# A feed-forward product as seven block products of sums instead of eight blocks, with two weight sums added up by the DMA

## The chip, the cores and the metric

The kernel runs on one core of a Trainium2 chip. A core has five engines that work side by side, each from its own in-order queue: TensorE (PE, matrix products; its weight loads are listed as PEld), VectorE (DVE), ScalarE (ACT), GpSimd (POOL) and SyncE (SP, which here only issues DMAs). Matrix products add into PSUM, eight banks of 128 x 512 float32; everything else lies in SBUF, 128 partitions wide. Engines wait for each other by semaphores. A DMA can be issued from SP, ACT or POOL.

The metric is device time in microseconds of one launch, lower is better.

## The reference

One layer of a diffusion backbone in float32: a token-mixing sub-layer with three mixers, then a gated feed-forward sub-layer, on 512 tokens of width 1024. The change lies in the feed-forward part:

```python
D_MODEL = 1024
D_FF = 2816      # ((8 * 1024 // 3 + 255) // 256) * 256

def swiglu(h, w_ffn_in, w_ffn_out):
    a, b = split_cols(h @ w_ffn_in, (D_FF, D_FF))
    return (jax.nn.silu(a) * b) @ w_ffn_out

h2 = rmsnorm(x, norm2_g) * (1 + sc2) + sh2          # (512, 1024)
x = x + g2 * swiglu(h2, w_ffn_in, w_ffn_out)        # w_ffn_in (1024, 5632), w_ffn_out (2816, 1024)
return rmsnorm(x, final_g)
```

## The kernel before

**Number format.** Matrix products run on float32r operands. To keep float32 accuracy each operand is split into a high and a low part (`split`, L142: ACT casts to the high part on L143, DVE subtracts it on L144), and a product is three matmuls: high x high, high x low, low x high (`mm3`, L254 to L257). The hidden state is split once; each weight tile is split after its load (`prep_w`, L146) into a pair `wh`, `wl`, of which there are two. So a third tile can be split only when the first has been used up.

**Weights.** A weight tile is 128 x 4 x 256: four blocks of 128 rows of the contraction, 256 output columns, 512 KB. `load_w` (L136, DMA on L139 by SP) brings it into one of three `wf` buffers.

**The stages around the change.** The output projection of the mixers (`gemm_tm` with `w_o`) yields token blocks m = 0 to 3, one after the other. For each, `residual` (L997) adds it to the stream `xr` and gets the norm's factor, DVE scales to `xn`, TensorE transposes `xn` (eight 128 x 128 transposes, L1032), and DVE and ACT evacuate the transposes with scale and shift (L1036, L1038). The result, features in the partitions and tokens along the free axis, is split into `h2h` and `h2l`.

**First feed-forward product.** Eleven groups g, each 256 columns of the gate half a and the matching 256 of the half b. A group takes four weight tiles (a or b, first or second half of the 1024 features), and each tile meets all 512 tokens: for two column blocks q and four row blocks kk three matmuls of 512 columns, 96 a group. Only group 0 is cut into two token halves with matmuls of 256 columns, since its second half of tokens comes last. ACT takes the SiLU of a from PSUM (L1077), DVE multiplies by b (L1078), and the product is split at once into `Ga` or `Gb`.

**Second feed-forward product.** `gemm_tm` with `w_ffn_out`: 22 row blocks k, each with a load, a scale by g2 (L154), a split and 24 matmuls. The final norm and the stores follow.

**Order.** Instructions are ordered when the program is built, by priorities: what stands under `prio("prep")` (loads, splits of weights) goes ahead as early as its buffers allow. On each engine the order is then fixed, and an instruction that waits holds up all behind it.

Of the kernel before, what the change touches and what calls it, by code (L numbers as in the profile page):

```python
# [9 lines left out]
F32 = mybir.dt.float32  # L10
# [64 lines left out]
def body(tc, I, out):  # L75
# [3 lines left out]
    with es:  # L79
# [22 lines left out]
        def gbank(name="g"):  # L102
            return psg.tile([128, 512], F32, name=name, tag="g")
# [703 lines left out]
        def cvf():  # L807
            return pF.tile([128, 512], F32, name="cvf", tag="cv", bufs=3)
# [212 lines left out]
        h2h = pH.tile([128, 8, 512], F32R, name="h2h", tag="hh")  # L1021
        h2l = pH.tile([128, 8, 512], F32R, name="h2l", tag="hl")
        for m, ps in gemm_tm(I["w_o"][0], g1b, lambda k, ms: (mh[:, k, ms], ml[:, k, ms]), 8, extra, 1):
            rs_ = residual(ps, xr, m, [xn[:, m % 2, 512 * n:512 * n + 512] for n in range(2)])
            V.tensor_scalar(out=xn[:, m % 2], in0=xr[:, m], scalar1=rs_, scalar2=None, op0=ALU.mult)
            for k4 in range(2):
                px = dbank()
                hf = cvf()
                p3, h3 = (t.rearrange("p (k j) -> p k j", k=4) for t in (px, hf))
                for kk in range(4):  # L1030
                    k = 4 * k4 + kk
                    T.transpose(p3[:, kk], xn[:, m % 2, 128 * k:128 * k + 128], ident)  # L1032
                for kk in range(4):
                    k = 4 * k4 + kk
                    if kk % 2:
                        A.activation(out=h3[:, kk], in_=p3[:, kk], func=AF.Identity, scale=a2[:, k:k + 1], bias=sh2[:, k:k + 1])  # L1036
                    else:
                        V.tensor_scalar(out=h3[:, kk], in0=p3[:, kk], scalar1=a2[:, k:k + 1], scalar2=sh2[:, k:k + 1], op0=ALU.mult, op1=ALU.add)  # L1038
                ms = slice(128 * m, 128 * m + 128)
                split(h3, h2h[:, 4 * k4:4 * k4 + 4, ms], h2l[:, 4 * k4:4 * k4 + 4, ms])  # L1040
        fstack.close()


        pG = es.enter_context(tc.tile_pool(name="pG", bufs=1))
        Ga = pG.tile([128, 18, 2, 512], F32R, name="Ga")
        Gb = pM.tile([128, 4, 2, 512], F32R, name="Gb", tag="M16")
        Gt = [Ga[:, k] for k in range(18)] + [Gb[:, k] for k in range(4)]
        gw = pM.tile([128, 2, 2, 4, 256], F32R, name="gw", tag="C16")
        wfi = I["w_ffn_in"][0].rearrange("(k p) f -> p k f", p=128)
        H2 = (lambda k: h2h[:, k], lambda k: h2l[:, k], 512, gbank)  # L1050
        cvg = lambda: pG.tile([128, 512], F32, name="cvg", tag="cv", bufs=3)
        for g in range(11):
            if g == 0:

                ab = [[gbank() for _ in range(2)], [gbank(), tbank()]]
                wts = []
                for i in range(2):
                    for half in range(2):
                        dst = None
                        if i:  # L1060
                            dst = [gw[:, half, p] for p in range(2)]
                        wts.append(prep_w(load_w(wfi[:, 4 * half:4 * half + 4, 2816 * i:2816 * i + 256]), dst=dst))
# [12 lines left out]
            for q in range(2):
                sa = cvg()
                A.activation(out=sa, in_=pa_[q], func=AF.Silu)  # L1077
                V.tensor_tensor(out=sa, in0=pb_[q], in1=sa, op=ALU.mult)  # L1078
                split(sa, Gt[2 * g + q][:, 0], Gt[2 * g + q][:, 1])
        fgb = pM.tile([128, 1024], F32, name="fgb", tag="C16")  # L1080
        GP.dma_start(out=fgb, in_=I["final_g"].partition_broadcast(128))
        yos = pH.tile([128, 4, 1024], F32, name="yos", tag="hh")
        ex = pH.tile([128, 2, 2, 4, 256], F32R, name="ex", tag="hl")
        extra = [(ex[:, i, 0], ex[:, i, 1]) for i in range(2)]
        for m, ps in gemm_tm(I["w_ffn_out"][0], g2b, lambda k, ms: (Gt[k][:, 0, ms], Gt[k][:, 1, ms]), 22, extra):
            yo = yos[:, m]
            rs_ = residual(ps, xr, m, [cvg() for _ in range(2)])
# [19 lines left out]
```

## Time and profile before

| | us |
|---|---|
| median of 3 runs | 975.82 (973.52 to 976.12) |
| profiled execution, its own time | 972.6 |
| its span, first to last instruction | 970.8 |
| first feed-forward product | 241.73 (601.20 to 842.93) |
| of it DVE busy, ACT busy | 88.67, 74.92 |
| second product and end, up to 963.80 | 120.87 |

The span is what the profile's rows cover; the execution's own time is a little longer. In a view of stretches a row gives the stretch, its length, and per engine the busy time with the number of instructions, then TensorE's granted clock, the DMA share and GB/s. In a timeline a row gives start, length, engine, line, operation, output and inputs, shape; a bracket tells how long the engine was idle before and who released it. In the view of groups the last numbers are total busy time, mean ns of one, and the idle time before. Matmuls overlap, so the time one costs in a stream is read from the distance between starts.

### The profile page before, as it was taken

What the parts mean: (1) busy time and instruction counts of PE and PEld (TensorE: products, weight loads), DVE (VectorE), ACT (ScalarE), POOL (GpSimd) and SP (SyncE); (2) the same over time, 40 slices, a digit from 0 to 9 for tenths busy, and PEclk for the clock granted to TensorE, in tenths of its full rate; (3) what the DMA queues carried; (4) which work ended last, traced back from release to release, by engine and by line L of the source; (5) the groups of instructions that cost most, each with busy time, mean ns of one, the idle gap of its engine ahead of it and who ended that gap; (6) DMA issues with size and microseconds to landing.
All of it is one profiled execution on the core that took longest, in us unless ns stands there. A gap on an engine that the chain in (4) does not pass through costs nothing.

```text
span 970.8 us, 14622 instructions
## 1 busy us (share of the span) xinstructions
PE 953.0 (98%) x5964; PEld 784.9 (81%) x5964; DVE 544.4 (56%) x880; ACT 417.9 (43%) x729; POOL 28.8 (3%) x47
## 2 busy tenths in 40 slices
PE   8999999899999999999999999999999999999997
PEld 7587887778788888888878888988888888888885
DVE  3575888369765423788874977333333333434455
ACT  5363884687863334362234346332323232211224
POOL 1002200000000000000000000000000000000000
PEclk9999999999999999999999999999999999999999
DMA  9820542512202232837774352223233333232322
GB/s 336 285 66 4 133 131 83 136 45 55 57 23 65 87 109 69 306 110 270 252 237 158 103 173 62 69 87 105 92 100 95 95 102 89 91 103 89 106 87 87
DMA packets 96836, 115.30 MB, mean 119 GB/s; under 512 B 18124, under 2 KB 84032, under 8 KB 96768
## 3 DMA queue, kind: packets, MB, share of 16 engines
q1 hardware_dynamic: 88192, 109.01, 35.5%
q0 software_dynamic: 1632, 3.44, 1.7%
q10 hardware_dynamic: 6944, 1.91, 0.8%
q8 instruction: 47, 0.77, 0.3%
q14 instruction: 21, 0.17, 0.1%
HBM read 110.58 MB, written 3.77 MB: 118 GB/s over the span
## 4 chain that ended last, share of the span: by engine, by line
PE 45%; DMA 3%; DVE 2%; issue 0%; ACT 0%; DVEq 0%
PE g L257 12%; PE g L256 12%; PE g L255 11%; PE d L257 2%; PE d L256 2%; PE d L255 2%; DMA wf<-in_w_ffn_out_dram 2%; DVE wl L144 1%; PE t L257 1%; PE t L256 1%; PE t L255 1%; DMA wm<-in_w_mod_dram 1%; DMA wf<-in_w_gate_dram 1%; DVE wf L154 1%; PE d L1032 0%
## 5 line engine op out<-in xcount | busy, mean ns | idle before, releaser
L144 DVE TENSOR_TENSOR wl<-wf,wh 128x1024 fp32r<-128x1024 f32 x131 | 160.0, 1222 | 214.4 <-ACT wh L143 213.7
L143 ACT CAST wh<-wf 128x1024 fp32r<-128x1024 f32 x131 | 137.8, 1053 | 299.1 <-PE g L256 161.5
L257 PE MATMUL g<-hh,wl 128*128 128x512 f32 x368 | 146.2, 397 | 0.3 <-DVE wl L144 0.3
L256 PE MATMUL g<-hl,wh 128*128 128x512 f32 x368 | 146.0, 397 | 0.0
L255 PE MATMUL g<-hh,wh 128*128 128x512 f32 x368 | 145.8, 396 | 0.0
L255 PE MATMUL g<-h2h,wh 128*128 128x512 f32 (+1 forms) x352 | 133.6, 380 | 0.0
L257 PE MATMUL g<-h2h,wl 128*128 128x512 f32 (+1 forms) x352 | 133.5, 380 | 0.0
L256 PE MATMUL g<-h2l,wh 128*128 128x512 f32 (+1 forms) x352 | 133.5, 379 | 0.0
L257 PEld LDWEIGHTS g<-hh,wl 128*128 128x128 f32 x368 | 69.6, 189 | 14.3 <-DVE wl L144 0.7
L256 PEld LDWEIGHTS g<-hl,wh 128*128 128x128 f32 x368 | 69.6, 189 | 14.1 <-issue 0.5
L255 PEld LDWEIGHTS g<-hh,wh 128*128 128x128 f32 x368 | 69.5, 189 | 13.6 <-issue 0.2
L256 PEld LDWEIGHTS g<-h2l,wh 128*128 128x128 f32 x352 | 66.2, 188 | 12.6
L255 PEld LDWEIGHTS g<-h2h,wh 128*128 128x128 f32 x352 | 66.2, 188 | 12.5
L257 PEld LDWEIGHTS g<-h2h,wl 128*128 128x128 f32 x352 | 66.1, 188 | 12.4
L154 DVE TENSOR_TENSOR wf<-wf,g2b 128x1024 f32<-128x1024 f32 x22 | 27.0, 1225 | 55.1 <-DMA wf<-in_w_ffn_out_dram 55.0
L830 DVE SCALAR_TENSOR_TENSOR acc<-wm,ct,acc 128x1024 f32<-128x1024 f32 x32 | 41.0, 1282 | 15.5 <-DMA acc<-in_b_mod_dram 7.3
L256 PE MATMUL d<-wl,Ga 128*128 128x512 f32 x72 | 28.0, 390 | 0.0
L257 PE MATMUL d<-wh,Ga 128*128 128x512 f32 x72 | 28.0, 389 | 0.0
L255 PE MATMUL d<-wh,Ga 128*128 128x512 f32 x72 | 28.0, 389 | 0.0
L713 ACT ACTIVATE SJ<-SJ,eGl 128x128 f32<-128x128 f32 x80 | 25.2, 403 | 3.9 <-PE d L701 3.5
L143 ACT CAST Ga<-cvg 128x512 fp32r<-128x512 f32 x18 | 11.1, 619 | 25.4 <-DVE cvg L1078 25.4
L256 PE MATMUL g<-wl,Ga 128*128 128x512 f32 x54 | 21.2, 393 | 0.1
(464 smaller groups left out, 1704.9 us busy)
## 6 DMA issues: line engine op xcount, KB each, us to landing
wm<-in_w_mod_dram SPq DMA_DIRECT2D x48, 512.0 KB, 5.5
wf<-in_w_ffn_in_dram SPq DMA_DIRECT2D x44, 512.0 KB, 3.5
wf<-in_w_in_dram SPq DMA_DIRECT2D x31, 512.0 KB, 3.9
wf<-in_w_gate_dram SPq DMA_DIRECT2D x24, 512.0 KB, 3.7
wf<-in_w_ffn_out_dram SPq DMA_DIRECT2D x22, 512.0 KB, 3.5
wf<-in_w_o_dram SPq DMA_DIRECT2D x8, 512.0 KB, 3.6
xl<-in_x_dram SPq DMA_DIRECT2D x4, 512.0 KB, 5.3
wf<-in_w_sc_out_dram SPq DMA_DIRECT2D x4, 512.0 KB, 3.3
```

What stands on the lines that cost most here:

```text
L143: A.copy(out=hi, in_=f)
L144: V.tensor_tensor(out=lo, in0=f, in1=hi.bitcast(F32), op=ALU.subtract)
L154: V.tensor_tensor(out=w, in0=w, in1=scale, op=ALU.mult)
L255: T.matmul(ps, lhsT=lh, rhs=rh, start=start, stop=False)
L256: T.matmul(ps, lhsT=lh, rhs=rl, start=False, stop=False)
L257: T.matmul(ps, lhsT=ll, rhs=rh, start=False, stop=stop)
L713: A.activation(out=S[:, u ^ par, h], in_=S[:, u ^ par, h], func=AF.Copy, scale=eGl[:, u, c_:c_ + 1])
L830: V.scalar_tensor_tensor(out=acc, in0=w, scalar=ct[:, k, 0:1], in1=acc, op0=ALU.mult, op1=ALU.add)
```

## The change

The product `w_ffn_in` x h2 of each group is treated as 2 x 2 blocks times 2 x 2 blocks. The weight blocks are A11, A12 (columns of a; first and second half of the features) and A21, A22 (columns of b). The activation blocks are B11, B21 (first 256 tokens; first and second half of the features) and B12, B22 (last 256 tokens). Instead of eight block products there are seven, of sums of blocks, each `prod` with 24 matmuls of 256 columns. In each group, in this order on TensorE:

| product | weight | activations | into |
|---|---|---|---|
| 1 | v = A11 | B11 | bank X |
| 2 | t = A21 + A22 | T1 = B12 - B11 | bank bA |
| 3 | t + v | T2 = B22 - T1 | bank bD |
| 4 | v + A21 | T3 = B12 - B22 | bank bB |
| 5 | A12 | B21 | bank X |
| 6 | t + v + A12 | -B22 | bank bA |
| 7 | A22 | T4 = B21 - T2 | bank bB |

The signs are as the code has them: c12 is stored negated and turned in its SiLU, and the products of c22 and c21 follow from it.

Weight sums: A21 + A22 and v + A21 are made by a DMA from POOL that adds into SBUF (`acc_w`, L1102); t + v and t + A12 by DVE (`add_w`, L1106), 128 x 1024 each. v and t exist twice, for even and odd groups. Loads per group rise from four tiles to six. The results are put together by seven DVE operations of 512 columns and four ACT operations, and the gated product is kept unsplit (`Gq`); it is split during the second product, into four slots `gs`. The sums of activations are made as the token blocks m = 2, 3 arrive (`sums_b`). For groups 0 and 1 products 1 and 5 run ahead of all others, since they need only the first 256 tokens.

```diff
+        def sums_b(h1, h2, js):
+            t1 = tmp()
+            V.tensor_tensor(out=t1, in0=h1, in1=Bf[:, 0:4, js], op=ALU.subtract)
+            split_b(t1, "T1", js)
+            t2 = tmp()
+            V.tensor_tensor(out=t2, in0=h2, in1=t1, op=ALU.subtract)
+            split_b(t2, "T2", js)
+            t3 = tmp()
+            V.tensor_tensor(out=t3, in0=h1, in1=h2, op=ALU.subtract)
+            split_b(t3, "T3", js)
+            V.tensor_tensor(out=Bf[:, 4:8, js], in0=Bf[:, 4:8, js], in1=t2, op=ALU.subtract)
+            nb = OB["nB22"]
+            A.activation(out=nb[:, 0, :, js], in_=h2, func=AF.Copy, scale=-1.0)
+            V.scalar_tensor_tensor(out=nb[:, 1, :, js], in0=h2, scalar=-1.0, in1=nb[:, 0, :, js].bitcast(F32), op0=ALU.mult, op1=ALU.subtract)
...
+        def prod(bank, w, b, first, last):
+            for q in range(2):
+                o, cs = bank[:, 256 * q:256 * q + 256], slice(128 * q, 128 * q + 128)
+                for kk in range(4):
+                    mm = ((w[0], b[:, 0]), (w[0], b[:, 1]), (w[1], b[:, 0]))
+                    for i, (l_, r_) in enumerate(mm):
+                        T.matmul(o, lhsT=l_[:, kk, cs], rhs=r_[:, kk], start=first and q == kk == i == 0, stop=last and kk == 3 and i == 2, skip_group_check=True)
+        def acc_w(w, src):
+            with prio("prep"):
+                GP.dma_start(out=w, in_=src, accum_op=ALU.add)
+        def add_w(w, other):
+            with prio("prep"):
+                V.tensor_tensor(out=w, in0=w, in1=other, op=ALU.add)
...
         for g in range(11):
-            if g == 0:
...
-                (pa_,) = gemm_fm(wfi[:, :, 256 * g:256 * g + 256], (H2,))
-                (pb_,) = gemm_fm(wfi[:, :, 2816 + 256 * g:2816 + 256 * g + 256], (H2,))
-            for q in range(2):
-                sa = cvg()
-                A.activation(out=sa, in_=pa_[q], func=AF.Silu)
-                V.tensor_tensor(out=sa, in0=pb_[q], in1=sa, op=ALU.mult)
-                split(sa, Gt[2 * g + q][:, 0], Gt[2 * g + q][:, 1])
+            v, t = vts[g % 2]
+            load_w2(wsrc(1, 0, g), t)
+            acc_w(t, wsrc(1, 1, g))
+            load_w2(wsrc(0, 0, g), v)
+            if g < 2:
+                X, e1 = Xs[g], e01[g]
+            else:
+                X, e1 = gbank(), e1g
+                prod(X, prep_w(v), OB["B11"], True, False)
+                A.copy(out=e1, in_=X)
+            bA = gbank()
+            prod(bA, prep_w(t), OB["T1"], True, False)
+            A.copy(out=e5, in_=bA)
+            add_w(t, v)
+            bD = dbank()
+            prod(bD, prep_w(t), OB["T2"], True, True)
+            V.tensor_tensor(out=u2, in0=bD, in1=e1, op=ALU.subtract)
+            acc_w(v, wsrc(1, 0, g))
+            bB = gbank()
+            prod(bB, prep_w(v), OB["T3"], True, False)
+            V.tensor_tensor(out=e57, in0=bB, in1=e5, op=ALU.add)
+            V.tensor_tensor(out=c22, in0=u2, in1=e57, op=ALU.add)
+            a12 = load_w(wsrc(0, 1, g))
+            if g >= 2:
+                prod(X, prep_w(a12), OB["B21"], False, True)
+            A.activation(out=sa0, in_=X, func=AF.Silu)
+            add_w(t, a12)
+            prod(bA, prep_w(t), OB["nB22"], False, True)
+            V.tensor_tensor(out=c12, in0=u2, in1=bA, op=ALU.add)
+            A.activation(out=sa1, in_=c12, func=AF.Silu, scale=-1.0)
+            prod(bB, prep_w(load_w(wsrc(1, 1, g))), OB["T4"], False, True)
+            V.tensor_tensor(out=c21, in0=u2, in1=bB, op=ALU.add)
+            V.tensor_tensor(out=Gq[g][:, :, 256:512], in0=q2(c22), in1=q2(sa1), op=ALU.mult)
+            V.tensor_tensor(out=Gq[g][:, :, 0:256], in0=q2(c21), in1=q2(sa0), op=ALU.mult)
...
-        for m, ps in gemm_tm(I["w_ffn_out"][0], g2b, lambda k, ms: (Gt[k][:, 0, ms], Gt[k][:, 1, ms]), 22, extra):
+        for m, ps in gemm_tm(I["w_ffn_out"][0], g2b, g_of, 22, extra):
```

The order on DVE inside the first product, before, over one group in the middle (`wl` is a weight split, `cvg` the product of the gate, `Ga` its split):

```order
L144 TENSOR_TENSOR wl_6071<-wf_6068,wh_6070 128x1024
L1078 TENSOR_TENSOR cvg_6056<-g_5994,cvg_6056 128x512
L144 TENSOR_TENSOR Ga_5703<-cvg_6056,Ga_5703 128x512
L1078 TENSOR_TENSOR cvg_6061<-g_5995,cvg_6061 128x512
L144 TENSOR_TENSOR wl_6101<-wf_6098,wh_6100 128x1024
L144 TENSOR_TENSOR Ga_5703<-cvg_6061,Ga_5703 128x512
L144 TENSOR_TENSOR wl_6133<-wf_6130,wh_6132 128x1024
L144 TENSOR_TENSOR wl_6163<-wf_6160,wh_6162 128x1024
```

And now, from the split for product 1 of group 3 to the split for its product 6 (`vt_5736` is v, `vt_5737` is t, `wf_6538` is A12; `Gq_5727` and the sum from `g_6286` belong to group 2; the rows of `tmps` that read `d_6476` and `g_6507` make u2 and e57):

```order
L144 TENSOR_TENSOR wl_6417<-vt_5736,wh_6416 128x1024
L1163 TENSOR_TENSOR Gq_5727<-tmps_5724 128x2x256
L1161 TENSOR_TENSOR tmps_5724<-tmps_5724,g_6286 128x512
L1164 TENSOR_TENSOR Gq_5727<-tmps_5724 128x2x256
L144 TENSOR_TENSOR wl_6447<-vt_5737,wh_6446 128x1024
L1106 TENSOR_TENSOR vt_5737<-vt_5737,vt_5736 128x1024
L144 TENSOR_TENSOR wl_6478<-vt_5737,wh_6477 128x1024
L1106 TENSOR_TENSOR vt_5737<-vt_5737,wf_6538 128x1024
L144 TENSOR_TENSOR wl_6509<-vt_5736,wh_6508 128x1024
L1146 TENSOR_TENSOR tmps_5724<-d_6476,tmps_5724 128x512
L144 TENSOR_TENSOR wl_6541<-wf_6538,wh_6540 128x1024
L1150 TENSOR_TENSOR tmps_5724<-g_6507,tmps_5724 128x512
```

What moved: four splits a group have become seven, the sum t + v (first L1106 row) stands behind the last sum and product of the group before and the split for product 2, and the split for product 4 (`wl_6509`) reads v after the DMA has added into it. The DMA is issued behind that first L1106 row.

The order on DVE at the start of the first product, before, from the last residual (`xr`) to the end of the splits of the last token block:

```order
L1003 TENSOR_TENSOR xr_5300<-xr_5300,d_5320 128x512
L144 TENSOR_TENSOR wl_5719<-wf_5716,wh_5718 128x1024
L144 TENSOR_TENSOR h2l_5312<-cvf_5618,h2h_5311 128x4x128
L1005 TENSOR_TENSOR n_r_5666<-n_s_5665 128x1
L144 TENSOR_TENSOR h2l_5312<-cvf_5630,h2h_5311 128x4x128
L1007 RECIPROCAL n_r_5666<-n_r_5666 128x1
L1025 TENSOR_SCALAR xn_5310<-xr_5300,n_r_5666 128x1024
```

And now, from the same residual to the same `xn` (`tb` are the sums T1 to T3 before their split, `ob` and `obt` the split parts):

```order
L1003 TENSOR_TENSOR xr_5300<-xr_5300,d_5322 128x512
L1038 TENSOR_TENSOR tb_5635<-cvf_5616,c16_5314 128x512
L1050 SCALAR_TENSOR_TENSOR ob_5312<-cvf_5626,ob_5312 128x4x128
L1041 TENSOR_TENSOR tb_5639<-cvf_5626,tb_5635 128x512
L144 TENSOR_TENSOR obt_5313<-tb_5635,obt_5313 128x4x128
L1047 TENSOR_TENSOR c16_5314<-c16_5314,tb_5639 128x4x128
L144 TENSOR_TENSOR obt_5313<-tb_5639,obt_5313 128x4x128
L1044 TENSOR_TENSOR tb_5643<-cvf_5616,cvf_5626 128x512
L1005 TENSOR_TENSOR n_r_5675<-n_s_5674 128x1
L144 TENSOR_TENSOR ob_5312<-tb_5643,ob_5312 128x4x128
L1007 RECIPROCAL n_r_5675<-n_r_5675 128x1
L1055 TENSOR_SCALAR xn_5310<-xr_5300,n_r_5675 128x1024
```

What moved: two splits and a weight split ahead of `xn` have become eight 512-wide operations. On TensorE the transposes of this `xn` stand behind product 1 of group 0, and ahead of product 1 of group 1.

More of the change, by code (lines that the diff above doesn't have):

```diff
@@ L1025, in body @@
             V.tensor_scalar(out=xn[:, m % 2], in0=xr[:, m], scalar1=rs_, scalar2=None, op0=ALU.mult)
+            js = slice(128 * (m % 2), 128 * (m % 2) + 128)
+            hs = []
             for k4 in range(2):
                 px = dbank()
-                hf = cvf()
-                p3, h3 = (t.rearrange("p (k j) -> p k j", k=4) for t in (px, hf))
+                p3 = px.rearrange("p (k j) -> p k j", k=4)
+                h3 = Bf[:, 4 * k4:4 * k4 + 4, js] if m < 2 else cvf().rearrange("p (k j) -> p k j", k=4)
+                hs.append(h3)
                 for kk in range(4):
@@ L1038, in body @@
                         V.tensor_scalar(out=h3[:, kk], in0=p3[:, kk], scalar1=a2[:, k:k + 1], scalar2=sh2[:, k:k + 1], op0=ALU.mult, op1=ALU.add)
-                ms = slice(128 * m, 128 * m + 128)
-                split(h3, h2h[:, 4 * k4:4 * k4 + 4, ms], h2l[:, 4 * k4:4 * k4 + 4, ms])
+                if m < 2:
+                    split_b(h3, ("B11", "B21")[k4], js)
+            if m >= 2:
+                sums_b(*hs, js)
         fstack.close()
         pG = es.enter_context(tc.tile_pool(name="pG", bufs=1))
-        Ga = pG.tile([128, 18, 2, 512], F32R, name="Ga")
@@ new lines, in prod @@
+        def prod(bank, w, b, first, last):
[4 more added lines that the diff above has]
+                    for i, (l_, r_) in enumerate(mm):
+                        T.matmul(o, lhsT=l_[:, kk, cs], rhs=r_[:, kk], start=first and q == kk == i == 0,
+                                 stop=last and kk == 3 and i == 2, skip_group_check=True)
@@ new lines, in acc_w, with load_w2, ahead @@
+        def acc_w(w, src):
[4 more added lines that the diff above has]
+                V.tensor_tensor(out=w, in0=w, in1=other, op=ALU.add)
+        def load_w2(src, w):
+            with prio("prep"):
+                SY.dma_start(out=w, in_=src)
+            return w
+        def ahead(g, e):
+            X = gbank()
+            prod(X, prep_w(load_w(wsrc(0, 0, g))), OB["B11"], True, False)
+            A.copy(out=e, in_=X)
+            return X
@@ L1080, in body, with g_of @@
+        gs = pM.tile([128, 4, 2, 512], F32R, name="gs", tag="M16")
+        halves_g = {}
+        def g_of(k, ms):
+            slot = gs[:, k % 4]
+            if k not in halves_g:
+                halves_g[k] = True
+                with prio("prep"):
+                    split(Gq[k // 2][:, k % 2], slot[:, 0], slot[:, 1])
+            return slot[:, 0, ms], slot[:, 1, ms]
         fgb = pM.tile([128, 1024], F32, name="fgb", tag="C16")
@@ L1084, in body @@
         extra = [(ex[:, i, 0], ex[:, i, 1]) for i in range(2)]
-        for m, ps in gemm_tm(I["w_ffn_out"][0], g2b, lambda k, ms: (Gt[k][:, 0, ms], Gt[k][:, 1, ms]), 22, extra):
+        for m, ps in gemm_tm(I["w_ffn_out"][0], g2b, g_of, 22, extra):
             yo = yos[:, m]
-            rs_ = residual(ps, xr, m, [cvg() for _ in range(2)])
+            rs_ = residual(ps, xr, m, [tmps[:, 2 * (m % 2) + i] for i in range(2)])
             V.tensor_tensor(out=yo, in0=xr[:, m], in1=fgb, op=ALU.mult)
```

51 lines of the change are left out of this document (27 added, 24 removed).

## The prediction

> **What bounds the kernel now.** I read the engine table first, then busy time by stage, then the matmuls by start time.
>
> ```profile
> span 970.8 us, 14622 instructions
> PE 953.0 (98%) x5964; PEld 784.9 (81%) x5964; DVE 544.4 (56%) x880; ACT 417.9 (43%) x729; POOL 28.8 (3%) x47
> ...
> 601.20:842.93 241.73, 241.73 (x1161) 204.21 (x1161) 88.67 (x100) 74.92 (x100) 0.54 (x1) 1.00 0.30 92
> ```
>
> TensorE is busy 98% of the span, and in the first feed-forward product (601.20 to 842.93) all of it, at granted clock 1.00. VectorE (DVE) and ScalarE (ACT) work 89 and 75 of those 242 us. TensorE alone sets this stage, so fewer columns streamed are a gain, as long as nothing else starts to set it. What a matmul costs is its start-to-start distance, not its listed duration (the listed ones overlap):
>
> ```profile
> 631.68 0.39 PE L255 MATMUL g<-h2h,wh 128*128 128x512 f32 x1
> ...
> 653.89 0.39 PE L257 MATMUL g<-h2h,wl 128*128 128x512 f32 x1
> 608.13 0.28 PE L257 MATMUL g<-h2h,wl 128*128 128x256 f32 x1
> ...
> 620.85 0.28 PE L255 MATMUL g<-h2h,gw 128*128 128x256 f32 x1
> ```
>
> 98 steps of 512 columns take 22.21 us, 0.2266 each; 106 steps of 256 columns (group 0 only) take 12.72, 0.1200 each. Half the columns cost 53%, each with a weight load of its own.
>
> **Term 1, the matmuls: -19 us.** Before: 10 groups of 96 matmuls at 0.2266 and 192 at 0.1200 make 240.6, and with eight transposes the stage's 241.7. After: 11 groups of 7 products, each of 2 x 4 x 3 = 24 matmuls of 256 columns, 2.88 us a product, 20.16 a group, 221.8 in all, 222.8 with the transposes. 1848 matmuls replace 1152, and the gain shrinks from an eighth to 19 us because of the 53%. Bounds 18 and 20; the row is of the same shape.
>
> **What feeds a product.** Each product needs a weight tile split by ACT (cast) and then by DVE (subtraction) into one of two buffer pairs. So the tile for product n+1 can be cast only when product n-1 has ended.
>
> ```profile
> L144 DVE TENSOR_TENSOR wl<-wf,wh 128x1024 fp32r<-128x1024 f32 x31 | 38.0, 1225 | 97.5 <-ACT wh L143 97.5
> L1078 DVE TENSOR_TENSOR cvg<-g,cvg 128x512 f32<-128x512 f32 x15 | 10.4, 691 | 9.6 <-PE g L257 9.6
> L143 ACT CAST wh<-wf 128x1024 fp32r<-128x1024 f32 x31 | 32.7, 1054 | 85.6 <-PE g L256 54.7 <-issue 30.9
> L1077 ACT ACTIVATE cvg<-g 128x512 f32<-128x512 f32 x16 | 9.5, 594 | 14.8 <-PE g L257 14.8
> ...
> 848.37 0.39 PE L257 MATMUL d<-wh,Ga 128*128 128x512 f32 x1
> 848.60 0.39 PE L255 MATMUL g<-wh,Ga 128*128 128x512 f32 x1
> 848.85 1.05 ACT L143 CAST wh<-wf 128x1024 fp32r<-128x1024 f32 x1 [3.61 <-PE d L257]
> ```
>
> The last two rows give the handover: the cast starts 0.25 us after the next block's first matmul. So 0.25 + 1.05 + 1.22 = 2.52 us after a product has started the next tile is split; 2.88 are there. Added DVE work per group: seven splits of 1.22, two sums of 1.22 (the shape of the split), seven 512-wide operations of 0.69: 15.8 of 20.16 us. ACT: seven casts and four 0.6 us operations, about 9.8. Both fit on average and cost nothing where they only fit between splits. If each product's split had also to stand behind one 0.69 us operation, six a group would be 0.33 late: that is the rival below.
>
> **Term 2, the wait for the accumulating DMA.** This is the step that I think decides. In a group, product 1 reads v, product 2 reads t, then DVE adds v to t (product 3), and only then may the DMA add the third block into v (product 4). Count from the start of product 1, when the last product of the group before has ended. DVE stands first at that group's last sum and multiplication (2 x 0.69, from 0.25: 1.6), then at the split for product 2 (2.85), then at t plus v (4.1). The DMA is issued and lands T later. Cast and split take 1.05 + 1.22 and 0.1 of handovers, less 0.24 since two matmuls need the cast alone: product 4 starts at 4.1 + T + 2.13. It is due after three products, at 8.64. The stall is T - 2.4 us a group. While DVE stands at the split for product 4 nothing behind it runs (the sum from product 3 and the split for product 5), but product 5 is needed only 2.88 us after product 4 starts, and both take 0.69 + 1.22: nothing more is lost. The DMA into t is issued a whole group ahead and is covered.
>
> T has no row, since no DMA of before accumulates. The nearest are in the view of DMA issues (KB each, median us from issue to landing); the last row is the page's line of bytes moved per slice:
>
> ```profile
> fgb<-in_final_g_dram POOLq DMA_DIRECT2D x1, 512.0 KB, 4.2
> wf<-in_w_ffn_in_dram SPq DMA_DIRECT2D x44, 512.0 KB, 3.5
> acc<-in_b_mod_dram POOLq DMA_DIRECT2D x4, 4.0 KB, 3.7
> GB/s 336 285 66 4 133 131 83 136 45 55 57 23 65 87 109 69 306 110 270 252 237 158 103 173 62 69 87 105 92 100 95 95 102 89 91 103 89 106 87 87
> ```
>
> The only plain 512 KB on the GpSimd queue took 4.2; it is the lower end. Accumulating has to read the destination as well: at the best slice's 336 GB/s another 512 KB take 1.56 us, so 5.8 with one such pass and 7.3 with two, my upper end. I take 5.0, halfway between the row and the row with one pass, nearer to the row since reads may overlap. Eleven groups x 2.6 = +28.6 us; with 4.2 it is +19.8, with 7.3 +53.9.
>
> **Term 3, the start: +8 us.** The block sums of the activations hang on DVE between the last residual and the first product. Before:
>
> ```profile
> 601.25 0.40 PE L257 MATMUL d<-wh,ml 128*128 128x512 f32 x1
> 601.48 0.27 PE L255 MATMUL g<-h2h,wh 128*128 128x256 f32 x1
> 606.54 1.04 PE L1032 MATMUL d<-cp,xn 128*128 128x128 f32 x8
> 601.83 0.68 DVE L1003 TENSOR_TENSOR xr<-xr,d 128x512 f32<-128x512 f32 x1
> 604.63 0.15 DVE L1005 TENSOR_TENSOR n_r<-n_s 128x1 f32<-128x1 f32 x1
> 605.69 0.75 DVE L1025 TENSOR_SCALAR xn<-xr,n_r 128x1024 f32<-128x1024 f32 x1
> 607.19 1.79 DVE L1038 TENSOR_SCALAR cvf<-d,a,sh 128x128 f32<-128x128 f32 x4 [0.75 <-PE d L1032]
> ```
>
> After, eight operations of 0.69 (three sums, the sum into B, -B22, three splits) and two of 0.15 stand between the residual's end (602.5) and xn, which starts at 608.4. Then follow xn 0.75, four evacuations 1.8, three weight splits 3.7, seven operations 4.8, and the split for group 0's product 2: 620.7. TensorE's work until there is four products ahead and eight transposes, 601.5 + 11.5 + 1.0 = 614.0. It is 6.7 us early. The next split stands behind 0.69 + 1.22 + 1.22 and takes 1.22, 4.35 against one product of 2.88: 1.4 more. Sum 8.1; bounds 2 (if ACT takes its share and the sums overlap) and 10.
>
> **Small terms, zero.** The splits of the gated product move from the first product to the second, where DVE then needs 2 x 1.22 + 0.69 = 3.1 us per row block and TensorE 24 x 0.2266 = 5.4; if that cover went, 22 x 0.69 = 15 us would show. SP's queue: six loads of 512 KB a group at 3.5, none later than its slot. At the join of the two products four of these splits stand ahead of group 10's product 6; 0.3 us, dropped.
>
> **Sum.** -18.9 + 28.6 + 8.1 = +17.8. The profiled execution took 972.6 (span 970.8 and 1.8 around it), 3.2 below the median of the runs; I keep that distance. After: 972.6 + 17.8 = 990.4 profiled, 993.5 as a median.
>
> **Rivals.**
>
> Faster: the DMA lands within 3.1 us. It is issued from DVE's sum and competes with one load at most; at T = 2.4 product 4 never waits and -18.9 + 8.1 = -10.8 gives 965; at 3.1 it is -3. It decides from T = 3.4, where the three terms cancel. Against it stands 4.2 for a transfer that reads no destination, and 3.7 for 4 KB. Chance 0.13.
>
> No change: T from 3.2 to 3.6, with 11 x 0.8 to 11 x 1.2, so -2 to +2.4: 974 to 978. Chance 0.07. [...]
>
> Much slower: the DMA takes 7.3 us or longer, since every row is read, added and written in turn. Then the stall is 4.9 or more, and -18.9 + 8.1 + 53.9 = +43: 1019 or above. For it: 512 rows of 1 KB instead of 128 of 4 KB. Against: the SP queue moves such rows in 3.5. Chance 0.14. [...] No stretch of this trace shows a clock under 0.997 in the mean.
>
> The split sets the pace: each product waits 0.33 for a split behind a 0.69 operation, 6 x 11 x 0.33 = 22 us, with a DMA that needs only 2.4. Then -18.9 + 8.1 + 22 = +11: 987. For it: 2.52 of 2.88 us are taken. Against: the operations that stand in front become ready with the cast and run beside its 1.05 us. Chance 0.06.
>
> That the change doesn't shorten TensorE's work could only be if 0.1200 did not hold; 106 steps say that it does.
>
> **Chances.** My forecast 0.60, with its own range from -18.9 + 2 + 19.8 = +3 to -18.9 + 10 + 53.9 = +45, 979 to 1021. The range over all takes in no change and part of the faster case: 969 to 1021. About 0.3% is what runs of this kernel tell from no change. Slower 0.60 + 0.14 + 0.06 = 0.80; same 0.07; faster 0.13.
>
> **What would show it.** Right: TensorE idle once a group, right before the product whose weights come from v, 2 to 4 us, ended by an ACT cast that waited for a DMA; T read directly as the landing of the two POOL transfers; one idle stretch of about 5 us before the last transposes at the start; 256-column matmuls 0.120 apart. Wrong: if the longest idle of ACT is not at that cast, or if TensorE stays over 97% busy in the stage, term 2 is wrong; if idle stretches of 0.3 us stand before each product, the split was it; if they are in the second product, the small terms were.

## The result, and the profile after

| | before | after |
|---|---|---|
| median of 4 runs, us | 975.97 (973.52 to 977.82) | 1034.28 (1028.61 to 1035.6) |
| profiled execution | 972.6 | 1028.61 |
| first feed-forward product | 241.73 | 299.90 |
| second product and end | 120.87 | 119.50 |

The ratio is 1.0586, 95% interval 1.0548 to 1.0624: the change makes the kernel 58 us slower, where 18 were forecast, and the time lies above the range. All of it is in the first feed-forward product.

The page of the changed kernel, its engine table and the row of granted clocks:

```profile
span 1026.6 us, 16340 instructions
PE 966.3 (94%) x6660; PEld 828.8 (81%) x6660; DVE 652.1 (64%) x1003; ACT 465.2 (45%) x789; POOL 57.1 (6%) x69
...
PEclk9999999999999999999999998998888998899999
```

The digits of the clock fall to 8 in the slices of the first product. The same two stages by stretches of time:

```profile
599.60:899.50 299.90, 256.46 (x1857) 248.27 (x1856) 186.19 (x207) 115.42 (x144) 27.48 (x22) 0.90 0.53 120
899.50:1019.00 119.50, 119.50 (x529) 98.69 (x529) 72.32 (x81) 40.88 (x60) 0.00 (x0) 1.00 0.31 95
```

TensorE is idle for 43 of the 300 us, and its mean clock there is 0.90 where it was 1.00. Two things cost, then: it stands, and when it runs it runs slower. The view of waits says at which products it stands (engine and tile, line; who released it, total us, times, longest), and what ACT stood for:

```profile
PE g L1097 <- ACT wh L143: 26.3, 11, 4.1
PE g L1097 <- DVE wl L144: 7.2, 11, 0.8
PE d L1065 <- DVE xn L1055: 4.5, 1, 4.5
PE d L1097 <- DVE wl L144: 4.4, 11, 0.8
...
ACT wh L143 <- DMA c<-in_w_ffn_in_dram: 26.1, 6, 5.0
ACT wh L143 <- DMA vt<-in_w_ffn_in_dram: 22.2, 5, 5.9
```

Eleven waits for the cast and eleven for the split before product 4 (tile `g`, one a group); eleven short ones for the split of t + v before product 3 (tile `d`); one at the start. ACT's eleven waits for a DMA are the accumulating ones. Group 2 in the timeline, from the sum t + v, behind which that DMA is issued, to product 4:

```profile
661.90 1.23 DVE L1106 TENSOR_TENSOR c<-c 128x1024 f32<-128x1024 f32 x1
663.66 1.28 POOL L1102 DMA_DIRECT2D c<-in_w_ffn_in_dram  x1 [4.96 <-ACT tmps L1139]
668.20 0.28 PE L1097 MATMUL d<-obt,wl 128*128 128x256 f32 x1
669.71 1.04 ACT L143 CAST wh<-c 128x1024 fp32r<-128x1024 f32 x1 [4.04 <-DMA c<-in_w_ffn_in_dram]
670.78 1.23 DVE L144 TENSOR_TENSOR wl<-c,wh 128x1024 fp32r<-128x1024 f32 x1 [4.00 <-ACT wh L143]
670.80 0.50 PE L1097 MATMUL g<-ob,wh 128*128 128x256 f32 x2 [2.33 <-ACT wh L143]
672.06 0.39 PE L1097 MATMUL g<-ob,wl 128*128 128x256 f32 x1 [0.76 <-DVE wl L144]
```

Product 3 issues its last matmul at 668.20, so product 4 is due at 668.32. It starts at 670.80, 2.48 late, and after two matmuls stands again until the split ends: 1.14 more. Then its stream runs slowly. The sum on DVE ends at 663.13, and the DMA is issued at 663.66, 0.53 later (the bracket names an ACT copy here; in nine of the eleven groups it names the sum). The group's product 4 starts at 670.80 and the next group's at 696.59, 25.8 apart; on the mean of eight groups the distance is 26.75, against 21.76 a group before and 20.16 of pure streaming. The view of DMA issues (KB each, median us to landing) has T:

```profile
c<-in_w_ffn_in_dram POOLq DMA_DIRECT2D x12, 512.0 KB, 6.2
vt<-in_w_ffn_in_dram POOLq DMA_DIRECT2D x10, 512.0 KB, 6.1
```

T is 6.1, not 5.0. And three stretches of 3 us behind this wait, in the order of the windows quoted before (the last three numbers are clock, DMA share, GB/s):

```profile
672.00:675.00 3.00, 2.94 (x16) 2.94 (x17) 1.74 (x3) 0.00 (x0) 0.00 (x0) 0.62 0.60 173
675.00:678.00 3.00, 3.00 (x23) 3.00 (x23) 1.47 (x3) 1.06 (x1) 0.00 (x0) 0.81 0.57 177
678.00:681.00 3.00, 3.00 (x28) 3.00 (x27) 1.72 (x2) 1.55 (x2) 0.00 (x0) 1.00 0.25 59
```

TensorE is busy all the time from 672 on, but issues 16 and 23 matmuls in 3 us, then 28: 0.38 x 3 + 0.19 x 3 = 1.7 us are lost to the clock after the wait has ended. The halved stretch (0.50) lasts 3.41 us here, from 672.75 to 676.16. From group 3 on it often lasts twice that (696.64 to 703.47 in group 3), part of it while TensorE still stands. Group 1 stood 2.14 and 0.76 us at its product 4, where the brackets of group 2 have 2.33 and 0.76, and kept a clock of 1.00.

### The profile page after: what moved, and what is told of

The parts are those of the page before. It is cut to its first block, busy times and chain, and to the rows that moved or that the text cites. A ratio compares the mean times of both kernels' runs of the same rounds, so it can differ in the third digit from the quotient of the medians.

```text
span 1026.6 us, 16340 instructions
## 1 busy us (share of the span) xinstructions
PE 966.3 (94%) x6660; PEld 828.8 (81%) x6660; DVE 652.1 (64%) x1003; ACT 465.2 (45%) x789; POOL 57.1 (6%) x69
## 5 line engine op out<-in xcount | busy, mean ns | idle before, releaser
L1097 PE MATMUL g<-ob,wh 128*128 128x256 f32 x880 | 181.4, 308 | 26.5 <-ACT wh L143 26.3
L1097 PEld LDWEIGHTS g<-ob,wh 128*128 128x128 f32 x880 | 155.1, 216 | 29.1 <-ACT wh L143 28.6
L1097 PE MATMUL g<-ob,wl 128*128 128x256 f32 x440 | 136.1, 309 | 7.2 <-DVE wl L144 7.2
L1097 PEld LDWEIGHTS g<-ob,wl 128*128 128x128 f32 x440 | 94.7, 215 | 9.9 <-DVE wl L144 9.9
L143 ACT CAST wh<-c 128x1024 fp32r<-128x1024 f32 x29 | 30.3, 1047 | 65.7 <-PE g L1097 29.9
L144 DVE TENSOR_TENSOR wl<-c,wh 128x1024 fp32r<-128x1024 f32 x29 | 35.5, 1223 | 34.9 <-ACT wh L143 34.9
L144 DVE TENSOR_TENSOR wl<-vt,wh 128x1024 fp32r<-128x1024 f32 x24 | 29.3, 1222 | 27.9 <-ACT wh L143 27.9
L1097 PE MATMUL d<-obt,wh 128*128 128x256 f32 x176 | 33.9, 291 | 0.9 <-ACT wh L143 0.9
L1097 PE MATMUL g<-obt,wh 128*128 128x256 f32 x176 | 32.2, 283 | 0.0
L255 PE MATMUL d<-wh,gs 128*128 128x512 f32 x80 | 31.1, 389 | 0.0
```

The lines of the kernel that those rows point to most:

```text
L143: A.copy(out=hi, in_=f)
L144: V.tensor_tensor(out=lo, in0=f, in1=hi.bitcast(F32), op=ALU.subtract)
L255: T.matmul(ps, lhsT=lh, rhs=rh, start=start, stop=False)
L1097: T.matmul(o, lhsT=l_[:, kk, cs], rhs=r_[:, kk], start=first and q == kk == i == 0, stop=last and kk == 3 and i == 2, skip_group_check=True)
```

## The experiments

Theory: the loss is the wait for the accumulating DMA before product 4, the clock that each wait costs, a short wait before product 3, and the start. Rivals: the seven products' other work (splits, sums on VectorE) would slow the stage without that DMA too; and, for T, that POOL's queue and not the accumulation is slow.

### The same transfer without accumulation

```diff
-            acc_w(v, wsrc(1, 0, g))
+            with prio("prep"):
+                GP.dma_start(out=v, in_=wsrc(1, 0, g))
```

> The DMA into v in front of product 4 overwrites v instead of adding to it; queue, waits and bytes stay (product 4 then uses A21 alone, so the sum v + A21 is left out). Theory A, the accumulation itself makes T long (6.1 us in the changed kernel) by its second read: T falls to 4.2 to 4.5, the stall before product 4 from about 3.7 to 1.8 to 2.1 us, too short for the clock to drop, and the time to -18.9 + 8 + 3 + 11 x 2 = about +14, 985 to 995. Theory B, it is the queue and the 512 rows of 1 KB (1.28 us of issue on POOL instead of 0.54): T stays at 5.5 to 6 and the time above 1020.

993.57 us, ratio 1.0191 (1.014 to 1.0242). The plain DMA stands on L1148; its issues and, at the end, least, median and longest landing:

```profile
L1148 POOL DMA_DIRECT2D c<-in_w_ffn_in_dram x6: 758/779/786, 628.3 to 848.2; - x6
...
DMA to landing us min/median/max: 3.8/3.8/5.7
```

The same 512 KB, from the same queue, into the same tile, issued behind the same sum: 3.8 us where accumulation takes 6.1, and 0.78 us to issue where it takes 1.28. T fell further than the 4.2 to 4.5 that were expected; the time of the two executions lies in its range. So POOL's queue is not slow, and the accumulating transfer costs 2.3 us more, 0.5 of them in the issue.

One thing changed beside the addition: the packets. The view of DMA queues (packets, MB, share of the time of 16 engines) for one transfer alone: the accumulating one of group 2 in the changed kernel (663.66 to 669.70), the plain one of this run (757.96 to 761.90), and a plain load from SP in the changed kernel (679.08 to 682.50).

```profile
q0 software_dynamic: 528, 0.52, 60.6%
...
q0 software_dynamic: 144, 0.52, 41.8%
...
q1 hardware_dynamic: 528, 0.52, 51.3%
```

Of each transfer's packets 16 are under 512 bytes. The others are its data: the accumulating transfer goes in 512 packets of 1 KB, the plain one from POOL in 128 of 4 KB. Share times 16 engines times length gives the engines' time: 59 us for the accumulating transfer, 26 for the plain one, and 28 for SP's load, which goes in the same 512 packets of 1 KB. So small packets alone don't double the time; with the addition a packet of 1 KB takes twice as long. What small packets would cost on POOL's own queue no run shows.

### The same from SP

```diff
-            acc_w(v, wsrc(1, 0, g))
+            load_w2(wsrc(1, 0, g), v)
```

> As the run before, but the overwriting DMA is issued from SP (the sum v + A21 is left out as well). Theory A and theory B: SP's loads of this shape land in 3.5, so T is 3.5 to 4, the stall 1.1 to 1.6 us, the clock stays at 1.00, the time 978 to 986. If the time stays above 1020, the stall has nothing to do with T.

983.04 us, ratio 1.0081 (1.0051 to 1.0111), mean clock 0.993. The time is as expected, the stall shorter than the 1.1 to 1.6. The wait before product 4 is down to one short piece: in groups 3 to 10 starts are 0.54 to 0.75 us apart at one place, instead of 0.12. So 51 us of the changed kernel's time hang on this one transfer. The kernel is still 7.6 us slower than the one before, though its matmuls save 18.9: some 26 us of other costs remain.

### Half of it

```diff
-            acc_w(v, wsrc(1, 0, g))
+            acc_w(v[:, 0:2], wsrc(1, 0, g)[:, 0:2])
```

> The changed kernel with only half of the third block added by the accumulating DMA into v (256 KB in place of 512; the other half of that sum is left out). Theory 'the accumulating transfer is paid by the byte' (6.1 us for 512 KB, of which about 2 do not depend on the size): issue to landing 4.0 to 4.3, idle time before product 4 down by about 2 us a group to 2.0 to 2.4, PE clock 0.99 or higher since the idle is short, time 990 to 1000. Rival 'it is a latency': landing 5.5 or longer, 1018 or more.

1002.29 us (1001.32 to 1004.59), ratio 1.0289 (1.0266 to 1.0312). The view of DMA issues:

```profile
c<-in_w_ffn_in_dram POOLq DMA_DIRECT2D x6, 256.0 KB, 4.5
vt<-in_w_ffn_in_dram POOLq DMA_DIRECT2D x5, 256.0 KB, 4.4
```

T falls by about 1.7 for 256 KB. If half the size saves half of what hangs on the size, some 2.8 us don't hang on it, an estimate from the two sizes; the 2 that I had put in was shown by no run. By that estimate more than half of the 6.1 us is paid by the byte or by the packet. The latency rival falls. The time misses by 2 us, and the clock didn't recover as expected (0.981 in the mean): behind the shorter waits it is still halved, though not each time. This is the most telling pair of rows of the study. Two groups of the same run, each with product 4's two waits (timeline), and for each group two windows of 3.41 us, the one in which the first wait lies and the next:

```profile
670.99 0.50 PE L1097 MATMUL g<-ob,wh 128*128 128x256 f32 x2 [0.82 <-ACT wh L143]
672.25 0.39 PE L1097 MATMUL g<-ob,wl 128*128 128x256 f32 x1 [0.76 <-DVE wl L144]
693.77 0.50 PE L1097 MATMUL g<-ob,wh 128*128 128x256 f32 x2 [0.79 <-ACT wh L143]
695.03 0.39 PE L1097 MATMUL g<-ob,wl 128*128 128x256 f32 x1 [0.76 <-DVE wl L144]
...
668.51:671.93 3.42, 2.16 (x16) 1.75 (x15) 0.96 (x1) 1.99 (x2) 0.00 (x0) 1.00 0.25 40
671.93:675.34 3.41, 3.09 (x25) 3.09 (x26) 2.15 (x4) 0.27 (x1) 0.00 (x0) 1.00 0.51 155
...
692.41:695.82 3.41, 1.86 (x13) 1.45 (x13) 2.07 (x3) 1.99 (x2) 0.00 (x0) 1.00 0.00 0
695.82:699.23 3.41, 3.41 (x18) 3.41 (x17) 0.89 (x1) 0.00 (x0) 0.00 (x0) 0.50 0.74 210
```

The same two waits, within 0.03 us, and the clock stays at 1.00 after one and is halved after the other. All halved stretches of this trace begin whole multiples of 3.41 us apart, so the windows are drawn at such a distance from 695.82. In the group that is halved both waits lie in one window; in the other the edge at 671.93 falls into the second wait. From group 2 on four of nine groups are halved.

### The wait filled with matmuls

```diff
-            prod(bD, prep_w(t), OB["T2"], True, True)
+            w3 = prep_w(t)
+            prod(bD, w3, OB["T2"], True, True)
+            fill = dbank()
+            for i in range(24):
+                kk, cs = i % 4, slice(128 * (i // 4 % 2), 128 * (i // 4 % 2) + 128)
+                T.matmul(fill[:, 0:256], lhsT=w3[1][:, kk, cs], rhs=OB["T2"][:, 1, kk], start=True, stop=True, skip_group_check=True)
```

> 24 matmuls of 256 columns (2.88 us) that nobody reads are put between product 3 and product 4 of every group, into a bank of their own, so that TensorE works while it waits; everything else stays. Clock theory: the stall itself is worth 11 x 3.7 us, but another 25 to 34 us of the loss come from the half clock that follows each stall. The filler takes no time of its own since product 4 waits for the DMA anyway, the granted clock stays at 1.00 and the time falls by 22 to 32 us, to 1002 to 1012. Rival, the slow matmuls behind the stall come from traffic or from late weights: the time stays within 5 us of 1034, or rises by up to 32.

1016.59 us (1014.76 to 1021.78), ratio 1.0421 (1.0385 to 1.0456). Eleven times 24 matmuls were added and the kernel became 17.7 us faster (the two sets of four executions lie 7 to 21 us apart), less than the 22 to 32 expected: product 4's weights come as late as before, only TensorE stands for little of that time. Nobody reads what the added matmuls make, so this is about the price of the clock behind these waits. One stretch in the run with the filler, and then the same in the changed kernel, clock third from the end:

```profile
700.00:800.00 100.00, 94.59 (x759) 92.75 (x758) 61.62 (x64) 37.76 (x44) 10.29 (x8) 0.98 0.56 124
```

```profile
700.00:800.00 100.00, 88.33 (x641) 86.11 (x640) 57.50 (x61) 35.70 (x42) 10.29 (x8) 0.88 0.53 119
```

0.98 against 0.88. 17.7 over eleven groups is 1.6 a group, and the windows of group 2 gave 1.7.

### Two products between product 3 and product 4

```diff
-            bB = gbank()
-            prod(bB, prep_w(v), OB["T3"], True, False)
-            V.tensor_tensor(out=e57, in0=bB, in1=e5, op=ALU.add)
-            V.tensor_tensor(out=c22, in0=u2, in1=e57, op=ALU.add)
             a12 = load_w(wsrc(0, 1, g))
...
             A.activation(out=sa1, in_=c12, func=AF.Silu, scale=-1.0)
+            bB = gbank()
+            prod(bB, prep_w(v), OB["T3"], True, False)
+            V.tensor_tensor(out=e57, in0=bB, in1=e5, op=ALU.add)
+            V.tensor_tensor(out=c22, in0=u2, in1=e57, op=ALU.add)
             prod(bB, prep_w(load_w(wsrc(1, 1, g))), OB["T4"], False, True)
```

> Products in the order 1, 2, 3, 5, 6, 4, 7, so that products 5 and 6 (5.76 us) stand between the issue of the DMA and its use; the DMA is unchanged, and the result is the same. Stall theory: product 4 is due at 14.4 us of the group and ready at 4.1 + 6.1 + 2.1 = 12.3, so the stall goes in groups 2 to 10 (groups 0 and 1 keep about 1 us), with it the half clock; -18.9 + 8 + 3 at the start + 2 + 11 x 0.3 = about -3: 968 to 980. Rival, the splits set the pace: 77 products at 0.33 us keep 20 us: 990 to 1000. Rival, nothing but bytes on the DMA queues: no change, 1034.

The order is 1, 2, 3, 5, 6, 4, 7, with the accumulating DMA as it is. 984.61 us (982.25 to 988.8), ratio 1.0104 (1.0067 to 1.0141): 49.7 us of the 58.3 are gone without a single operation less. It is some 5 us above the range that was expected. The waits:

```profile
PE g L1097 <- DVE tmps L1158: 8.8, 10, 0.9
PE d L1097 <- DVE wl L144: 3.6, 10, 0.8
```

None is for product 4's weights any more. A new one has come: product 7 now stands right behind product 4, adds into the same bank, and must wait for VectorE's read of it (1.03 late by start times, ten groups). The wait before product 3 is still there, 0.58 late. A steady group takes 21.82 us = 20.16 + 0.58 + 1.03 and 0.05.

### An order without neighbours

The order is 1, 2, 5, 3, 7, 4, 6; product 7 gets a bank of its own, bC, and the sums are taken up in another order, with as many operations.

```diff
             add_w(t, v)
+            acc_w(v, wsrc(1, 0, g))
+            a12 = load_w(wsrc(0, 1, g))
+            if g >= 2:
+                prod(X, prep_w(a12), OB["B21"], False, True)
...
             prod(bD, prep_w(t), OB["T2"], True, True)
...
+            bC = dbank()
+            prod(bC, prep_w(load_w(wsrc(1, 1, g))), OB["T4"], True, True)
             bB = gbank()
-            prod(bB, prep_w(v), OB["T3"], True, False)
+            prod(bB, prep_w(v), OB["T3"], True, True)
+            V.tensor_tensor(out=w24, in0=u2, in1=bB, op=ALU.add)
+            V.tensor_tensor(out=c21, in0=w24, in1=bC, op=ALU.add)
+            V.tensor_tensor(out=c22, in0=w24, in1=e5, op=ALU.add)
             prod(bA, prep_w(t), OB["nB22"], False, True)
```

> Order of the products 1, 2, 5, 3, 7, 4, 6 in place of 1 to 7: no product stands right behind one that must end before its own weight sum can start, product 4 comes four products after product 2, and product 7 has a bank of its own (its sum is then made of two reads). Work on every engine as in the changed kernel. Theory 'the waits for sums and their clock are the whole loss of the steady groups': no PE idle over 0.3 us in a steady group, period 20.2 us against 26.75 in the changed kernel, clock 0.99 or higher, time 967 to 972 (984.6 of the order 1,2,3,5,6,4,7, less nine groups x 1.66), a little below the kernel before. Rival 'the splits set the pace': 0.3 us or more before most products whatever the order, period 21 or longer, 977 or more.

974.26 us (971.5 to 979.05), ratio 0.9998 (0.998 to 1.0016): no difference from before, 2 us above what was expected. The steady groups do what the theory says. Windows of this run:

```profile
625.00:650.00 25.00, 22.45 (x168) 21.86 (x168) 16.87 (x18) 8.52 (x11) 3.85 (x3) 0.93 0.92 204
650.00:700.00 50.00, 47.62 (x382) 47.42 (x383) 35.30 (x37) 21.82 (x25) 5.11 (x4) 0.97 0.71 170
700.00:800.00 100.00, 100.00 (x835) 100.00 (x835) 75.62 (x81) 47.14 (x55) 12.86 (x10) 1.00 0.70 156
```

From 700 on TensorE is busy 100%, clock 1.00, 835 matmuls in 100 us (0.120 each), with VectorE at 76%: the rival in which the splits set the pace falls for the steady groups. What is left lies ahead of 700, in groups 0 and 1, whose products 1 and 5 are done ahead, so that nothing is left to put between. There product 3 stands right behind product 2 and product 4 three products after it: starts are 0.77 to 2.71 us apart in five places between 624 and 653, three of them at product 3 and two at product 4 of group 1, seven us in all, and the clock falls with them.

### The start

`sums_1` makes T1 and T2, `sums_2` T3, the update of B21 and -B22; they run when the loop over token blocks has ended, and the first operation of block 2 takes a value of block 3's xn, by two copies of one column each. The split of T4 moves into group 0.

```diff
             if m >= 2:
-                sums_b(*hs, js)
+                held.append((*hs, js, xn[:, 1, 0:1] if m == 2 else None))
+        t2s = [sums_1(*h) for h in held]
+        for (h1, h2, *r), t2 in zip(held, t2s):
+            sums_2(h1, h2, t2, *r)
```

> The changed kernel, with the block sums of the third row block of activations held back until the fourth row block has been scaled (xn), and the split of the fourth sum moved into group 0. Same work. Theory 'the position of the sums costs the start': PE's wait of 4.46 us before the last transposes falls to about 1.5, the first product of group 0 starts 3 to 5 us earlier, time 1026 to 1031. Rival 'the amount of VectorE work costs the start' (VectorE is idle only 2.8 us between 600 and 624): the wait only moves to before product 2 of group 0, gain under 1.5 us: 1033 or more.

1036.44 us, ratio 1.0643 (1.0614 to 1.0673): nothing won, perhaps something lost. The transposes now come in time, and the wait stands behind them (lines are ten lower in this kernel):

```profile
608.90 1.06 PE L1072 MATMUL d<-cp,xn 128*128 128x128 f32 x8 [0.27 <-DVE xn L1062]
613.43 0.80 PE L1107 MATMUL g<-ob,wh 128*128 128x256 f32 x2 [3.46 <-ACT wh L143]
```

4.46 us of wait became 0.27, and 3.46 appeared one step on, since the held-back sums and casts now stand ahead of the next weight tile's cast on ACT and split on DVE. Further on, product 4 of group 0 stands 5.57 us for its transfer. This speaks for the rival, that at the start the amount of work decides and not its place; no other place was tried.

> Both: the order 1, 2, 5, 3, 7, 4, 6 and the sums held back. If the two costs add, the time is that of the order alone less the 3 to 5 us of the start: 963 to 968, 0.8% to 1.3% below the kernel before. If VectorE's amount of work decides at the start, it is that of the order alone, 967 to 972.

Both edits together: 977.89 us (974.12 to 980.86), ratio 1.0021 (0.9997 to 1.0045), 3.6 us above the order alone and above both ranges that were expected. Like the run before, it shows no gain from holding the sums back.

### The first two groups as a pair

`group(g)` is the loop's body with a yield behind each product, so groups 0 and 1 run 2, 2, 3, 3, 7, 7, 4, 4, 6, 6; the others in the order 1, 2, 5, 3, 7, 4, 6.

```diff
-        for g in range(11):
+        pair = [group(g) for g in range(2)]
+        for _ in range(5):
+            for p_ in pair:
+                next(p_, None)
+        for g in range(2, 11):
+            for _ in group(g):
+                pass
```

> The order 1, 2, 5, 3, 7, 4, 6 for groups 2 to 10, and the first two groups, whose products 1 and 5 are done ahead, run as a pair: 2, 2, 3, 3, 7, 7, 4, 4, 6, 6. Theory 'what the order alone left (974.3) are the waits of the first two groups': six idle stretches of 0.99 to 2.71 us between 624 and 653 less 0.12 each, 7.0 us, and a clock of 0.93 to 0.97 there, 3 to 4 us. With twice the distance they go: no PE idle over 0.8 us after the four products ahead, time 962 to 968, 0.7% to 1.3% below the kernel before. Rival 'VectorE's backlog from the activation sums must be paid there in any order', as in the run with the sums held back: the idle time comes up at other products of the pair, 971 or more.

984.92 us, ratio 1.0087 (1.0056 to 1.0118): 10.7 us slower than the order alone. The time lies in the rival's range, but the reason is a third one:

```profile
624.13 0.92 SPq L1110 DMA_DIRECT2D vt<-in_w_ffn_in_dram  x2
628.99 1.28 POOL L1102 DMA_DIRECT2D vt<-in_w_ffn_in_dram  x1 [2.33 <-ACT Gq L1141]
636.93 1.04 ACT L143 CAST wh<-vt 128x1024 fp32r<-128x1024 f32 x1 [8.63 <-DMA vt<-in_w_ffn_in_dram]
638.02 0.80 PE L1097 MATMUL g<-obt,wh 128*128 128x256 f32 x2 [10.85 <-ACT wh L143]
```

Group 1's t is loaded at 624 only, because its tile lies in space that the activations' buffers hold until then: SP waits 3.1 us for DVE's operation on L1050, which reads one of them. In the order by groups, group 0's five products hide that; in the pair, group 1's product 2 is the second. The other accumulation, the one that the prediction called covered, then stands in the open: load, 7.9 us of adding in this place, cast.

> The same with four of the 128 x 512 sums of activations (the difference for T3 and the update of B21, two row blocks each) on GpSimd in place of VectorE: four times about 0.6 us less on VectorE at the start. If VectorE's amount of work at the start sets how late the last transposes and product 2 are, PE's wait of 4.46 us falls to 3.3 or less and the time is 1 to 3 us below that of the pair alone. Rival: GpSimd takes so long for one that T3 and its readers are late, or VectorE is slowed beside it: same time or longer.

The same with four sums on GpSimd: 984.27 us, ratio 1.0086 (1.0055 to 1.0117), no different from the pair (984.92). The groups on POOL:

```profile
L1044 POOL TENSOR_TENSOR tb<-cvf 128x512 f32<-128x512 f32 x2 | 3.3, 1666 | 8.9 <-DVE tb L1041 8.9
L1047 POOL TENSOR_TENSOR c<-c,tb 128x512 f32<-128x512 f32 x2 | 2.9, 1432 | 43.4 <-DVE tb L1041 43.4
```

GpSimd takes 1.4 to 1.7 us for what VectorE does in 0.69, and the wait at the transposes fell only from 4.46 to 3.81. With the long wait of the pair behind it the run can't tell whether that would be worth anything elsewhere; this stays open.

### The pair, mended

Group 1's two weight tiles lie in space that is free early, and the pair runs 2, 2, 3, 3, 6, 6, 4, 4, 7, 7.

```diff
-        vts = [pre, [pG.tile([128, 4, 256], F32, name="vt", tag=f"vt{i}") for i in range(2)]]
+        vts = [pre, [pF2.tile([128, 4, 256], F32, name="vt", tag=t_) for t_ in ("u", "gt")]]
...
+            if g < 2:
+                p6()
+                yield
+                p4()
+                yield
+                sums(p7())
```

> The pair again, mended by what its trace shows: group 1's two weight tiles lie in space that is free before the activations' buffers are given back (there PE stood 11.1 us for t of group 1, which could only be loaded after that), and the pair's order is 2, 2, 3, 3, 6, 6, 4, 4, 7, 7, so that t and v of group 0 come free earlier for group 2 (2.6 and 1.3 us there). If those transfers were the whole of the pair's loss, PE has no idle over 1 us between the four products ahead and the second feed-forward product, and the time is 984.9 - 11.0 - 3.6 - about 4 of clock (0.73 in the 25 us of that stretch) = 964 to 968. Rival: VectorE's backlog comes up behind the products ahead, several us idle before product 2: 972 or more.

965.26 us (961.36 to 966.97), against 975.92 for the kernel before beside it: ratio 0.9876, interval 0.9857 to 0.9896. It is as expected, and faster than both kernels. The page and windows:

```profile
PE 938.5 (97%) x6660; PEld 805.8 (84%) x6660; DVE 651.2 (67%) x1003; ACT 465.3 (48%) x789; POOL 57.1 (6%) x69
...
600.00:625.00 25.00, 20.22 (x136) 19.04 (x135) 22.31 (x37) 15.68 (x30) 0.14 (x1) 0.86 0.20 64
625.00:650.00 25.00, 23.99 (x201) 23.79 (x200) 20.29 (x21) 13.42 (x16) 4.95 (x4) 1.00 0.91 211
650.00:700.00 50.00, 50.00 (x416) 49.76 (x415) 39.13 (x43) 22.46 (x26) 6.11 (x5) 1.00 0.67 157
```

The same 6660 matmuls, 1003 DVE and 789 ACT operations as the changed kernel, the same accumulating transfers, 69 us less. From 650 to 700, where the order without neighbours still ran at 0.97, TensorE is busy throughout at 1.00. Only the start's wait of 4.5 us is left among the long ones. The tiles and the pair's order were changed together, so what each is worth stays open.

## Why the prediction was wrong

**The bound and term 1: right.** The streamed matmuls are 0.120 us apart (835 in a window of 100 us where nothing waits), and the gain of 18.9 us is there: the mended order ends 965.26 - (975.92 - 18.9) = 8.2 us above the time that term 1 alone would give.

**Term 3, the start: right in size by luck.** Those 8.2 us are what is left when the other long waits are gone; 8.1 was forecast, as 6.7 of wait before the last transposes and 1.4 at a later split. The idle stretch before the transposes is there, but 4.46 us long. Most of the rest is the clock again, which that term didn't have: 0.86 over 600 to 625 in the mended run, at most 3.5 us.

**Term 2, the mechanism right, the size too small.** The wait is where it was put and ends as it was said to, with an ACT cast that waited for a DMA. The filler run and the order 1, 2, 3, 5, 6, 4, 7 differ by 32.0 us; the second has 10.3 us of a new wait, so the waits before product 4 cost some 42. In group 2 they were 2.48 + 1.14, which makes 40 in eleven. Product 3 adds 0.58 a group, 6.4 in all: t + v ends at 4.1 us after product 1's start by the prediction's own count, cast and split take 1.05 + 1.22, 6.4, and product 3 is due at 5.76. The prediction didn't name that wait, but its stall is counted from the start of product 1 and so takes it in: a late product 3 only moves a part of the stall forward, as the DMA doesn't hang on it. So some 48 us stand against the 28.6 of the sum.

The step that failed is the choice of T: "halfway between the row and the row with one pass, nearer to the row since reads may overlap". T was 6.1 and not 5.0, which is 12 us over eleven groups. A plain transfer from the same queue takes 3.8, the difference of 2.3 holds 0.5 of issue, and the other 1.8 is a little more than one full pass at 1.56. The packets, twice as long with the addition, fit with a pass that isn't overlapped, but no run shows the reads by themselves. A second step failed beside it: "The DMA is issued and lands T later" puts nothing between DVE's sum and the issue. There are 0.53 us in group 2, about 6 over the eleven. T - 2.4 with T = 6.1 is 3.7 a group, 40.7 in all; with these 6 it is some 47, close to the 48.

"Nothing more is lost" held: behind product 4, product 5 doesn't wait.

**What was left out of the sum: the clock, about 17.7 us.** The sum has no term for it, and the prediction says "No stretch of this trace shows a clock under 0.997 in the mean". That reading is wrong. The trace of the kernel before shows the half clock (0.50) twice, once at 83.84 to 87.25 and once at its end, behind a stretch in which TensorE stands:

```profile
964.50:967.89 3.39, 0.00 (x0) 0.00 (x0) 1.96 (x5) 1.74 (x4) 0.00 (x0) 1.00 0.04 13
967.89:970.80 2.91, 0.00 (x0) 0.00 (x0) 0.00 (x0) 0.00 (x0) 0.00 (x0) 0.50 0.43 165
```

At its end it costs nothing, as no matmul follows. What it costs behind the waits of the changed kernel, the filler run measures: 17.7 us, 1.6 a group. In the changed kernel the halved stretches of the first product (0.50) last 3.41 us or twice that and begin whole multiples of 3.41 us apart. In the run with half the transfer, two waits of 0.79 and 0.76 us, with two matmuls between, were followed by one, and waits of 0.82 and 0.76 us in the group before were not. What decides between the two, no run shows.

**The sum.** -18.9 + 48.4 + 17.7 + 8.2 is 55.4, against 58.3 measured. The rest of some 3 us is not assigned. In the trace product 3 of group 0 stands longer than the others, and so does product 4 of group 5, whose transfer took 7.2 us, but no run isolates them.

**The rivals.** "Much slower" came out in its range, 1019 or above, and with a longer T, but T was 6.1 and not the 7.3 that it asked for: it took the clock on top to get there. "The split sets the pace" was refuted by the run without neighbours, where TensorE is busy 100% beside the same splits. The rival "no change" asked for a T of 3.2 to 3.6, which is below both rows: 3.8 plain, 6.1 accumulating.

## What to carry to other kernels

When a change adds a chain (sum, transfer, cast, split) ahead of a product, place it by distance: write down for each product when its operand can be ready at the earliest, and put independent products between. Here the same operations took 1034, 985 or 974 us by order alone, and 965 with two buffers moved as well. Count a long wait on TensorE twice, once for its length and once for the halved clock behind it: here waits of 2 to 5 us before product 4 were followed by it in ten of eleven groups, at some 1.6 us each, and waits of about 2 us in four of nine. If no other work can fill the wait, even useless matmuls do: here eleven times 24 of them made the kernel 17.7 us faster. And when an order is changed, look again at what the old order had hidden: a second accumulation, a bank's reader, a late buffer.

## What the runs showed of the hardware

A DMA that adds into SBUF took 6.1 us for 512 KB, in 512 packets of 1 KB, and 4.4 to 4.5 for 256 KB, where a plain one from the same queue took 3.8 for 512 KB, in 128 packets of 4 KB; POOL is held 1.28, 1.19 and 0.78 us by the issue. The addition doubled the DMA engines' time against a plain load in the same packets (59 and 28 us). POOL issued the DMA 0.53 us after the DVE operation that it waited for had ended. The clock was halved (0.50) behind standing that was neither long nor in one piece: 0.79 and 0.76 us in one group, while 0.82 and 0.76 us in the one before it left it at 1.00. The halved stretches in the first product of the changed kernel began whole multiples of 3.41 us apart. A 128 x 512 float32 sum takes GpSimd 1.4 to 1.7 us and VectorE 0.69.
